# Searching the key lists of all tokens while the queries are made, with 96 instead of 100 first products ahead of the gates

## The chip, the cores and the metric

The kernel runs on one core of a Trainium2 chip, in one launch. The metric is the device time of one execution in microseconds, and the number that counts is the median of several runs. The core has five engines: TensorE (PE in the profile, its weight loads PEld), VectorE (DVE), ScalarE (ACT), GpSimd (POOL) and SyncE (SP), and 16 DMA engines that move data between DRAM and the core's own memory.

## The reference

The function is two transformer blocks on 512 tokens of width 1024, in float32. The first block (attention in a window and a convolution, then a gated feed-forward layer) and the first half of the second (a sparse attention and a spatial gate) are not touched by the change. What matters is the last layer, `peer`, a mixture of 16384 tiny experts:

```
q    = (xn @ wq).reshape(bsz, s, 8, 2, 128)
sub  = einsum('bshpd,hpnd->bshpn', q, subkeys)       # 16 lists of 128 key scores per token
s_top, i_top = top_k(sub, 16)                         # the best 16 of each list
cand = s_top[..., 0, :, None] + s_top[..., 1, None, :]
best, pos = top_k(cand, 16)                           # the best 16 of 256 sums per head
expert = i_top of half 0 * 128 + i_top of half 1, at pos
gate = softmax(best)
a = gelu(x . u_tab[expert]);   y = sum(gate * a * v_tab[expert])
```

Each token thus has 8 heads x 16 = 128 experts out of 16384, and each expert is one row of `u_tab` and one row of `v_tab`, 1024 numbers each.

## The kernel before

Matrix products run in three passes: each operand is split into a rounded part (`whi`, a cast on ScalarE, L138) and the rest (`wlo`, a subtraction on VectorE, L140), and `mm3` (L155 to L158) multiplies high by high, low by high and high by low. `unit` (L132) loads one 128x1024 block of weights on SyncE's queue into `raw` and makes the two parts; all three tiles come from rings of four buffers.

The `peer` layer treats the tokens in two ways. Tokens 0 to 319 (`N_U` = 320) are computed densely: for each of the 128 blocks of 128 experts, `u_block` (L939) forms the first product of all 320 tokens with the block's rows of the first table (8 x 3 matmuls of 320 columns) and applies gelu. The gates for all experts, mostly zero, are built as a dense matrix by `build` (L1091), in 16 steps per 128 tokens: one-hot tiles made by VectorE, multiplied on TensorE (L1117). Later the gated activations of a block meet the block's rows of the second table in `v_block` (L1243), 18 matmuls of 512 columns, the second product. Tokens 320 to 511 are computed sparsely: `gathered` (L954) fetches one row per token and expert by an indirect DMA on GpSimd's queue, and VectorE multiplies and sums it; 64 gathers serve tokens 320 to 383, whose gates are then folded into the dense matrix, and 128 gathers of each table serve tokens 384 to 511.

The layer runs in three stages.

The query stage (L1179 to L1193) is a loop over four rounds (`c4`) of four chunks (`j`). Each chunk is one 128-wide piece of the queries for all 512 tokens (24 matmuls) and its scores against the keys (`skT`). At the end of a round the scores of four lists for each of the four groups of 128 tokens (`tb` 0 to 3) are copied out of the banks to `sub`. `top_keys` (L976) searches one list of one token group: five VectorE instructions over 128x128 scores.

The second stage is the loop of first products made ahead of the gates (L1196 to L1204): `NSPILL` = 100 blocks, chosen by `SPAIR` as pairs spread over the 64 pairs, with the first three pairs left out. Every four results go to DRAM (`a_dram`) and are read back later. Beside them the routing work is issued.

The third stage makes the second products, pair by pair. For a pair in `SPAIR` the first products are read back; for another they are made there and then. The first second product needs the finished gates; the first products of the two opening pairs need none and can run before.

The order of the work is set by generators. `routed` (L1156) yields, after each small piece of routing work, a charge in microseconds; `advance` (L245) draws pieces until a given amount is spent, and stops early at a charge of zero. In the query stage each chunk of rounds 1 to 3 draws `TOP_US`; beside each first product `R_US` is drawn, of which, once the expert numbers of tokens 256 to 383 are known (`ready`), `GATHER` x 2 goes to gathers, and `GATHER` x 1 after the first 64 gathers are issued (`made2`). A search is charged 1.6, `keys` of a group 21.2 (18.7 for the last tokens), a build step 2.7 or 3.4, a gather 1.3. `keys` (L988) selects the best 16 sums of a head and finds the expert numbers; it needs all 16 lists of its group. `routed` takes the lists of `tb` 2 and 3 from `todo` as they come, then runs `keys` of 2 and 3, then searches the 32 lists of `tb` 0 and 1, then `keys` and `build` of 0 and 1, then `build` of 2. What of it is left after the loop is issued behind it (L1205). In the third stage each second product draws `G_US` of gathers, and half as much again where the pair makes its first products there.

The compiler that places the instructions keeps each engine's stream in the order of issue where it can, and lets a later instruction go first where its inputs are ready sooner; searches and the sums over gathered rows are tied behind the last `wlo` issued before them (`pace`).

Of the kernel before, what the change touches and what calls it, by code (L numbers as in the profile page):

```python
# [21 lines left out]
NEG = -1.0e30  # L22
GBUFS = 7

TOP_US = 5.0

R_US = 3.6
GATHER = 0.5
G_US = 2.3
NSPILL = 100  # L30
N_PE_TAPS = (0, 0, 8, 8)
N_GATE = 5
SA_BUFS = 7
# [10 lines left out]

SPAIR = [N_HEAD + i for i in range(64 - N_HEAD) if i * NSPILL // 2 // (64 - N_HEAD) != (i + 1) * NSPILL // 2 // (64 - N_HEAD)]
MAGIC = 1.5 * 2.0 ** 23
# [14 lines left out]
def tile_layers(ctx: ExitStack, tc: tile.TileContext, A: dict, out: bass.AP):  # L61
# [3 lines left out]
    def pool(name, bufs=1, stack=ctx, **kw):  # L65
        return stack.enter_context(tc.tile_pool(name=name, bufs=bufs, **kw))
# [8 lines left out]
    def bank(tag):  # L75
        return ps.tile([128, 512], F32, tag=tag, name="bank_" + tag)
# [51 lines left out]
    def order(ins):  # L128

        return tc.issue_after(ins) if ins is not None else ExitStack()  # L130
# [15 lines left out]
    def next_unit(n=1024, after=(None, None)):  # L146
        u = unit(wt[wpos[0]], n, after)
        wpos[0] += 1
        return u
# [46 lines left out]
    def proj_T(u, xhi, xlo, nk=8, c0=0, o=None):  # L196

        o = bank("a") if o is None else o
        for k in range(nk):
            mm3(o, u[0][:, c0 + k * 128:c0 + (k + 1) * 128], u[1][:, c0 + k * 128:c0 + (k + 1) * 128],  # L200
                xhi[:, :, k, :], xlo[:, :, k, :], k == 0, k == nk - 1)
        return o
# [28 lines left out]
    def chain(*gs):  # L231
        for g_ in gs:
            yield from g_
# [11 lines left out]
    def advance(gen, us):  # L245
        while us > 0:
            c = next(gen, None)
            if c is None:
                return 0.0
            if c == 0.0:  # L250
                return 0.0
            us -= c
        return us
# [685 lines left out]
    def u_block(i1, ap, tag):  # L939

        u = unit(A["ut"][i1])
        o = bank(tag)[:, :N_U]
        for k in range(8):
            mm3(o, u[0][:, k * 128:(k + 1) * 128], u[1][:, k * 128:(k + 1) * 128],
                xhi8[:, k, 0:N_U], xlo8[:, k, 0:N_U], k == 0, k == 7)
        S.activation(ap, o, AF.Gelu_apprx_tanh)
# [29 lines left out]
    def top_keys(sub, tb, hps):  # L976
        sv, si = tops[tb]
        for hp in hps:
            x = sub[:, hp, :]
            with order(pace[0]):  # L980
                V.max(out=sv[:, hp, 0:8], in_=x)
                V.max_index(out=si[:, hp, 0:8], in_max=sv[:, hp, 0:8], in_values=x)
                V.match_replace(out=x, in_to_replace=sv[:, hp, 0:8], in_values=x, imm_value=-3.0e38)
                V.max(out=sv[:, hp, 8:16], in_=x)
                V.max_index(out=si[:, hp, 8:16], in_max=sv[:, hp, 8:16], in_values=x)
            yield 1.6
# [92 lines left out]
    def weights2():  # L1079

        S.activation(zg[64:128, 0:64], ga2[64:128], AF.Gelu_apprx_tanh)
        S.activation(zg[0:64, 64:128], ga2[0:64], AF.Gelu_apprx_tanh)
        zp = bank("b")[:, 0:64]
        T.matmul(zp, zg, fold, start=True, stop=True)
        V.tensor_tensor(gT2, zp, gT2, op=OP.mult)
        for j in range(3):
            V.tensor_copy(w2s[:, j], gT2)
            if j < 2:
                V.tensor_tensor(gT2, gT2, w2s[:, j], op=OP.subtract)
# [38 lines left out]
    with ExitStack() as st:  # L1128
        ptop = pool("ptop", stack=st)
        sTs = {tb: ptop.tile([128, 4, 128], F16, name=f"sT{tb}") for tb in (0, 2)}  # L1130
        sTs[1] = sTs[0]
        gT2 = ptop.tile([128, 64], F32, name="gT2")
        w2s = ptop.tile([128, 3, 64], BF16, name="w2s")
        zg = ptop.tile([128, 128], F32, name="zg")
        G.memset(zg, 0.0)
        fold = ptop.tile([128, 64], F32, name="fold")
        V.tensor_tensor(fold, ident[:, 0:64], ident[:, 64:128], op=OP.add)
        turn16 = ptop.tile([128, 128], F16, name="turn16")
        V.tensor_copy(turn16.rearrange("p (a t) -> p a t", a=2), ident[:, None, 64:128].to_broadcast([128, 2, 64]))
        tops = [(ptop.tile([128, 16, 16], F32, name=f"sv{tb}"), ptop.tile([128, 16, 16], U32, name=f"si{tb}")) for tb in range(4)]  # L1140
        iota16 = ptop.tile([128, 128, 2], F16, name="iota16")
        V.tensor_copy(iota16, cst[:, C_IOTA:C_IOTA + 128][:, :, None].to_broadcast([128, 128, 2]))
        iotab = ptop.tile([128, 16, 128], F16, name="iotab")
        V.tensor_copy(iotab, cst[:, C_IOTA:C_IOTA + 16][:, :, None].to_broadcast([128, 16, 128]))
        ident16 = ptop.tile([128, 128], F16, name="ident16")
        V.tensor_copy(ident16, ident)
        st2 = ExitStack()
        pk = pool("pk", stack=st2)

        sub = [gres[tb].rearrange("p s i t -> p (s i t)")[:, 0:2048].rearrange("p (a n) -> p a n", a=16) if tb < 2 else  # L1150
               pk.tile([128, 16, 128], F32, name=f"sub{tb}") for tb in range(4)]
        skT = pk.tile([128, 16, 128], F32, name="skT")
        nc.scalar.dma_start(skT, A["skT"])
        todo = []

        def routed():  # L1156
            while todo or not keyed:
                if todo:
                    yield from todo.pop(0)
                else:  # L1160
                    yield 0.0
            st2.close()
            pr = pool("pr", stack=st)
            yield from keys(pr, 2)
            yield from keys(pr, 3)
            for tb in (0, 1):
                yield from top_keys(sub[tb], tb, range(16))
            for tb in (0, 1):
                yield from keys(pr, tb)
                yield from build(pr, tb)  # L1170
            while not made2:
                next(gat)
            weights2()
            yield 0.5
            yield from build(pr, 2)

        keyed = []
        route = routed()
        d1 = d2 = 0.0  # L1179
        for c4 in range(4):  # L1180
            sb_ = [bank("b") for _ in range(4)]
            for j in range(4):
                hp = c4 * 4 + j
                qc = pk.tile([128, 512], F32, name="qc", bufs=2)
                S.copy(qc, pr4[j] if c4 == 0 else proj_T(next_unit(), xhi, xlo))
                for tb in range(4):
                    T.matmul(sb_[tb][:, j * 128:(j + 1) * 128], qc[:, tb * 128:(tb + 1) * 128], skT[:, hp, :],
                             start=True, stop=True)
                if c4:
                    d1 = advance(route, d1 + TOP_US)  # L1190
            for tb in range(4):
                S.copy(sub[tb][:, c4 * 4:c4 * 4 + 4, :], sb_[tb].rearrange("p (a n) -> p a n", a=4))
            todo += [top_keys(sub[tb], tb, range(c4 * 4, c4 * 4 + 4)) for tb in (2, 3)]  # L1193
        keyed.append(True)
        for n4 in range(0, 2 * len(SPAIR), 4):
            ab = ptop.tile([128, 4, N_U], F32, name="ab", bufs=2)  # L1196
            for j in range(4):
                u_block(2 * SPAIR[(n4 + j) // 2] + j % 2, ab[:, j, :], "a")

                if ready:  # L1200
                    g1 = GATHER * (2 - len(made2))
                    d2 = advance(gat, d2 + g1)
                d1 = advance(route, d1 + R_US - (g1 if ready else 0.0))
            nc.scalar.dma_start(a_dram[n4 // 4], ab)  # L1204
        for _ in route:  # L1205
            pass
# [196 lines left out]
```

## Time and profile before

| | |
|---|---|
| median of the runs shown | 2115.23 us |
| runs | 2115.23, 3382.32, 2110.91 us |
| profiled execution | 2110.76 us |
| its span, first to last instruction | 2109.0 us |
| mean granted clock of TensorE | 0.989 of full speed |
| busy: TensorE, weight loads, VectorE | 2049.5, 1745.1, 1571.4 us |
| busy: ScalarE, GpSimd | 824.6, 517.9 us |
| DMA | 476.66 MB, mean 226 GB/s |

The profile is one execution; all its times are microseconds from its first instruction. The query stage runs from about 930 to 1025, the second stage from there to about 1465, the third to 2105. A matmul counts as busy until its modelled end, and the next one starts before that, so the distance between starts is the better measure of TensorE's pace. One run of the three, 3382.32 us, is far from the other two.

### The profile page before, as it was taken

What the parts mean: (1) busy time and instruction counts of PE and PEld (TensorE: products, weight loads), DVE (VectorE), ACT (ScalarE), POOL (GpSimd) and SP (SyncE); (2) the same over time, 40 slices, a digit from 0 to 9 for tenths busy, and PEclk for the clock granted to TensorE, in tenths of its full rate; (3) what the DMA queues carried; (4) which work ended last, traced back from release to release, by engine and by line L of the source; (5) the groups of instructions that cost most, each with busy time, mean ns of one, the idle gap of its engine ahead of it and who ended that gap; (6) DMA issues with size and microseconds to landing.
All of it is one profiled execution on the core that took longest, in us unless ns stands there. A gap on an engine that the chain in (4) does not pass through costs nothing.

```text
span 2109.0 us, 29481 instructions
## 1 busy us (share of the span) xinstructions
PE 2049.5 (97%) x11112; PEld 1745.1 (83%) x11112; DVE 1571.4 (75%) x2881; ACT 824.6 (39%) x1339; POOL 517.9 (25%) x383
## 2 busy tenths in 40 slices
PE   7999999999999999999999999999999999999999
PEld 6747888888887777898889899999888878788887
DVE  7974633332279854455789999998899888899997
ACT  5454433222254342333443455555333333233332
POOL 1000000000011000000032212121566666576663
PEclk9999999999999999999999999999999999999999
DMA  5302323333232212342378899999999999999996
GB/s 183 101 21 80 100 93 98 100 112 98 71 104 87 80 59 87 104 145 80 110 282 276 288 326 331 311 359 300 394 399 410 388 400 395 410 395 410 411 404 237
DMA packets 163377, 476.66 MB, mean 226 GB/s; under 512 B 13934, under 2 KB 57326, under 8 KB 161314
## 3 DMA queue, kind: packets, MB, share of 16 engines
q1 hardware_dynamic: 67104, 259.70, 34.5%
q0 software_dynamic: 46752, 169.36, 21.2%
q10 hardware_dynamic: 49378, 45.71, 6.4%
q8 instruction: 87, 1.43, 0.3%
q14 instruction: 56, 0.46, 0.1%
HBM read 431.99 MB, written 42.47 MB: 225 GB/s over the span
## 4 chain that ended last, share of the span: by engine, by line
PE 58%; DVE 26%; issue 6%; DMA 4%; POOL 2%; ACT 2%; DVEq 0%; POOLq 0%; ACTq 0%; SPq 0%
PE bank_a L158 13%; PE bank_a L157 13%; PE bank_a L156 13%; DVE wlo L140 6%; PE bank_b L156 4%; PE bank_b L157 4%; PE bank_b L158 4%; DVE rows L966 2%; DVE rows L958 2%; DMA rows<-in_peer_u_dram,gidx 2%; POOL rows L950 2%; DMA al<-a_dram 1%; DVE mask L708 1%; DVE ohh L1110 1%; DVE oh L1104 1%
## 5 line engine op out<-in xcount | busy, mean ns | idle before, releaser
L138 ACT CAST whi<-raw 128x1024 fp32r<-128x1024 f32 (+1 forms) x413 | 431.9, 1047 | 885.0 <-PE bank_a L157 325.9
L140 DVE TENSOR_TENSOR wlo<-raw,whi 128x1024 fp32r<-128x1024 f32 (+1 forms) x413 | 500.4, 1214 | 268.0 <-ACT whi L138 263.5
L158 PE MATMUL bank_a<-xhi,wlo 128*128 128x320 f32 (+2 forms) x1600 | 545.6, 341 | 5.7 <-DVE wlo L140 3.6
L156 PE MATMUL bank_a<-xhi,whi 128*128 128x320 f32 (+2 forms) x1600 | 549.6, 344 | 1.4 <-issue 1.0
L157 PE MATMUL bank_a<-xlo,whi 128*128 128x320 f32 (+2 forms) x1600 | 546.7, 342 | 2.5 <-DVE xlo L153 2.2
L950 POOL DMA_INDIRECT rows<-in_peer_u_dram,gidx x192 | 277.3, 1444 | 560.4 <-DVE gidx L1051 145.2
L158 PEld LDWEIGHTS bank_a<-xhi,wlo 128*128 128x128 f32 x1600 | 302.3, 189 | 34.7 <-DVE wlo L140 6.3
L157 PEld LDWEIGHTS bank_a<-xlo,whi 128*128 128x128 f32 x1600 | 302.9, 189 | 29.5 <-DVE xlo L153 3.3
L156 PEld LDWEIGHTS bank_a<-xhi,whi 128*128 128x128 f32 x1600 | 302.2, 189 | 28.9 <-issue 2.3
L950 POOL DMA_INDIRECT rows<-in_peer_v_dram,gidx x128 | 205.5, 1606 | 116.4 <-DVE h L973 92.5
L156 PE MATMUL bank_a<-whi,wvhi 128*128 128x512 f32 x512 | 202.0, 394 | 6.3 <-ACT wvhi L152 6.2
L158 PE MATMUL bank_a<-whi,wvlo 128*128 128x512 f32 x512 | 201.6, 394 | 2.4 <-DVE wvlo L153 2.3
L157 PE MATMUL bank_a<-wlo,wvhi 128*128 128x512 f32 x512 | 201.6, 394 | 1.7 <-DVE wlo L140 1.7
L973 DVE SCALAR_TENSOR_TENSOR h<-rows,ga,h 128x1024 f32<-128x1024 f32 x128 | 164.4, 1284 | 5.1 <-DMA rows<-in_peer_v_dram,gidx 3.5
L173 POOL TENSOR_TENSOR rstd<-rstd,neghalf 128x1 f32<-128x1 f32 x20 | 12.2, 612 | 614.1 <-DVE rstd L172 614.1
L966 DVE SCALAR_TENSOR_TENSOR rows<-rows,h 128x1024 f32<-128x1024 f32 x128 | 152.8, 1220 | 8.7 <-DMA rows<-in_peer_u_dram,gidx 8.6
L156 PEld LDWEIGHTS bank_a<-whi,wvhi 128*128 128x128 f32 x512 | 97.0, 189 | 27.6 <-ACT wvhi L152 8.3
L158 PEld LDWEIGHTS bank_a<-whi,wvlo 128*128 128x128 f32 x512 | 97.1, 190 | 26.7 <-DVE wvlo L153 6.1
L157 PEld LDWEIGHTS bank_a<-wlo,wvhi 128*128 128x128 f32 x512 | 97.0, 189 | 21.6 <-DVE wlo L140 2.4
L156 PE MATMUL bank_b<-whi,wvhi 128*128 128x512 f32 x256 | 99.6, 389 | 0.0
L158 PE MATMUL bank_b<-whi,wvlo 128*128 128x512 f32 x256 | 99.6, 389 | 0.0
L157 PE MATMUL bank_b<-wlo,wvhi 128*128 128x512 f32 x256 | 99.6, 389 | 0.0
(402 smaller groups left out, 3269.0 us busy)
## 6 DMA issues: line engine op xcount, KB each, us to landing
raw<-in_wt_dram SPq DMA_DIRECT2D x150, 512.0 KB
raw<-in_ut_dram SPq DMA_DIRECT2D x128, 512.0 KB
raw<-in_peer_v_dram SPq DMA_DIRECT2D x128, 512.0 KB
g_dram<-gt ACTq DMA_DIRECT2D x24, 896.0 KB
gl<-g_dram SPq DMA_DIRECT2D x14, 1536.0 KB
a_dram<-ab ACTq DMA_DIRECT2D x25, 640.0 KB
al<-a_dram SPq DMA_DIRECT2D x25, 640.0 KB
rows<-in_peer_u_dram,gidx POOLq DMA_INDIRECT x192
```

Of the source, the lines that this page charges most:

```text
L138: lead[0] = S.copy(hi[:, :n], raw[:, :n]).ins
L140: pace[0] = V.tensor_tensor(lo[:, :n], raw[:, :n], hi[:, :n].bitcast(F32), op=OP.subtract).ins
L156: T.matmul(o, lh, rh, start=start, stop=False)
L157: T.matmul(o, lh, rl, start=False, stop=False)
L158: T.matmul(o, ll, rh, start=False, stop=stop)
L708: V.match_replace(out=sc, in_to_replace=m8, in_values=sc, imm_value=-3.3e38)
L950: G.indirect_dma_start(out=r, out_offset=None, in_=table, in_offset=bass.IndirectOffsetOnAxis(ap=idx[:, k:k + 1], axis=0))
L958: V.scalar_tensor_tensor(r, r, 1.0, hn2, op0=OP.mult, op1=OP.mult, accum_out=ga2[:, k:k + 1])
L966: V.scalar_tensor_tensor(r, r, 1.0, hn3, op0=OP.mult, op1=OP.mult, accum_out=ga[:, k:k + 1])
L973: V.scalar_tensor_tensor(h[3], r, ga[:, k:k + 1], h[3], op0=OP.mult, op1=OP.add)
L1104: V.tensor_tensor(oh2, io, part(sT[:, 1], t0), op=OP.is_equal)
L1110: V.tensor_tensor(o_, oh2, x_, op=OP.mult)
```

## The change

Four constants change, and the list of waiting searches becomes two lists. After each round the searches of `tb` 2 and 3 go to `todo[0]` and those of `tb` 0 and 1 to `todo[1]`, in pieces of two lists. `routed` draws from the first and, where that is empty, from the second, until the queries are made and the first list is empty; what is then left of the second runs where all 32 searches of `tb` 0 and 1 ran, behind `keys` of 2 and 3. Two pairs leave `SPAIR`, so four first products are made in the third stage.

```diff
-TOP_US = 5.0
-
-R_US = 3.6
-GATHER = 0.5
+TOP_US = 8.0
+
+R_US = 3.3
+GATHER = 0.6
 G_US = 2.3
-NSPILL = 100
+NSPILL = 96
...
-        todo = []
+
+        todo = [[], []]
 
         def routed():
-            while todo or not keyed:
-                if todo:
-                    yield from todo.pop(0)
+            while todo[0] or not keyed:
+                if todo[0] or todo[1]:
+                    yield from (todo[0] or todo[1]).pop(0)
                 else:
                     yield 0.0
             st2.close()
             pr = pool("pr", stack=st)
             yield from keys(pr, 2)
             yield from keys(pr, 3)
-            for tb in (0, 1):
-                yield from top_keys(sub[tb], tb, range(16))
+            yield from chain(*todo[1])
             for tb in (0, 1):
                 yield from keys(pr, tb)
                 yield from build(pr, tb)
...
-            todo += [top_keys(sub[tb], tb, range(c4 * 4, c4 * 4 + 4)) for tb in (2, 3)]
+            for tb in (2, 3, 0, 1):
+                todo[tb < 2] += [top_keys(sub[tb], tb, range(c4 * 4 + j, c4 * 4 + j + 2)) for j in (0, 2)]
```

`chain` runs generators one after the other.

## Rows read from the trace of the kernel before

**Rows 1.** The page's first part: busy us, share of the span, instructions.

```profile
PE 2049.5 (97%) x11112; PEld 1745.1 (83%) x11112; DVE 1571.4 (75%) x2881; ACT 824.6 (39%) x1339; POOL 517.9 (25%) x383
```

**Rows 2.** Table by stretches: length, busy us (instructions), granted clock, DMA share, GB/s.

```profile
core 0: us, PE busy (x) PEld busy (x) DVE busy (x) ACT busy (x) POOL busy (x), PEclk, DMA share, GB/s
945.00:971.00 26.00, 26.00 (x125) 21.18 (x124) 13.32 (x68) 7.09 (x11) 0.00 (x0) 1.00 0.23 77
1045.00:1085.00 40.00, 33.73 (x231) 31.63 (x231) 35.05 (x133) 17.17 (x24) 13.05 (x12) 0.87 0.74 264
1125.00:1225.00 100.00, 94.10 (x674) 90.33 (x673) 99.37 (x337) 44.06 (x65) 22.57 (x20) 1.00 0.83 281
1225.00:1465.00 240.00, 236.13 (x2070) 230.63 (x2068) 234.76 (x414) 136.96 (x250) 49.66 (x39) 0.99 0.97 332
1478.00:2105.00 627.00, 616.60 (x2884) 518.77 (x2883) 570.20 (x648) 211.78 (x238) 384.52 (x240) 0.99 0.98 389
```

**Rows 3.** Timeline of TensorE: start, duration, operation; first and last of even sequences.

```profile
1431.06 0.23 PE L1117 MATMUL bank_b<-oh,ohh 128*128 128x128 f16 x1
...
1432.40 0.22 PE L1117 MATMUL bank_b<-oh,ohm 128*128 128x128 f16 x1
...
1466.10 0.31 PE L156 MATMUL bank_b<-xhi,whi 128*128 128x320 f32 x1
...
1466.98 0.31 PE L156 MATMUL bank_b<-xhi,whi 128*128 128x320 f32 x1
...
1478.42 0.40 PE L156 MATMUL bank_a<-whi,wvhi 128*128 128x512 f32 x1
...
2077.77 0.39 PE L156 MATMUL bank_a<-whi,wvhi 128*128 128x512 f32 x1
...
2079.13 0.39 PE L156 MATMUL bank_b<-whi,wvhi 128*128 128x512 f32 x1
```

**Rows 4.** Timeline of VectorE: two bursts of searches, the first one's end, build operations.

```profile
973.33 0.49 DVE L981 MAX8 sv<-sub 128x8 f32<-128x128 f32 x2 [1.40 <-ACT sub L1192]
...
982.70 2.34 DVE L140 TENSOR_TENSOR wlo<-raw,whi 128x1024 fp32r<-128x1024 f32 x2
...
1025.41 0.49 DVE L981 MAX8 sv<-sub 128x8 f32<-128x128 f32 x2 [1.40 <-ACT sub L1192]
...
1215.70 0.69 DVE L1103 TENSOR_TENSOR oh<-iota,sT 128x1024 f16<-128x1024 f16 x1
...
1216.91 0.69 DVE L1110 TENSOR_TENSOR ohl<-oh,sT 128x1024 f16<-128x1024 f16 x1
```

**Rows 5.** Groups of VectorE instructions, 1025 to 1465: busy us, mean ns, idle before.

```profile
L140 DVE TENSOR_TENSOR wlo<-raw,whi 128x1024 fp32r<-128x1024 f32 x100 | 121.2, 1213 | 4.8 <-ACT whi L138 2.4 <-issue 2.3
L958 DVE SCALAR_TENSOR_TENSOR rows<-rows,h 128x1024 f32<-128x1024 f32 x64 | 77.5, 1214 | 2.0 <-DMA rows<-in_peer_u_dram,gidx 1.9
...
L966 DVE SCALAR_TENSOR_TENSOR rows<-rows,h 128x1024 f32<-128x1024 f32 x6 | 7.3, 1219 | 0.0
```

**Rows 6.** Waits from 930 to 1025: us in total, times, longest.

```profile
DVE wlo L140 <- ACT whi L138: 42.8, 11, 5.3
```

**Rows 7.** Waits from 1025 to 1478.

```profile
ACT whi L138 <- DMA raw<-in_ut_dram: 25.3, 11, 4.1
...
PE bank_b L1043 <- DVE ohl L1040: 7.5, 5, 2.5
```

**Rows 8.** Table by stretches again, three short ones with full DMA engines.

```profile
1250.00:1300.00 50.00, 50.00 (x407) 49.28 (x406) 50.00 (x127) 28.68 (x49) 12.96 (x10) 1.00 1.02 364
1075.00:1085.00 10.00, 6.96 (x24) 5.94 (x25) 7.74 (x24) 2.77 (x4) 5.32 (x5) 0.67 1.03 413
...
1835.00:1850.00 15.00, 10.75 (x35) 7.62 (x34) 14.91 (x14) 5.58 (x7) 9.59 (x6) 0.77 1.03 399
```

**Rows 9.** Waits from 1478 to 2105.

```profile
ACT whi L138 <- DMA raw<-in_peer_v_dram: 104.8, 36, 7.2
...
DVE gl L1237 <- DMA al<-a_dram: 20.3, 5, 4.9
```

## The prediction

> **What bounds the kernel now.** I read the page first: TensorE counts as busy for 97% of the span, VectorE for 75% [rows 1], so only time in which TensorE waits can be won. The table by stage then says where VectorE presses on it [rows 2]. While the queries are made (945 to 1025) TensorE is busy without a gap and VectorE about half the time: 13.32 of 26 us. From 1025 to 1465, the stage of the first products made ahead, VectorE is busy 99.37 of 100 us in the middle and 234.76 of the 240 behind it, and TensorE's gaps lie there. From 1478 on TensorE is at 616.60 of 627 and the DMA engines at 0.98.
>
> A busy share hides spacing, so I priced TensorE by the distance of starts [rows 3]. 320-column products start 0.88 us apart over six, 0.147 each; 512-column ones 1.36 over six, 0.227; the 128-column f16 ones of the gate building 1.34 over 23, 0.058. One first product (24 matmuls) is then 3.52 us. From 1025.4, just behind the last query round, to the first second product at 1478.42 lie 104 of them (100 ahead and four of the two opening pairs), 832 gate matmuls and some 160 of `keys`: 366.1 + 48.3 + 9.3 = 423.7 of 453.0 us. TensorE loses 29 us there. From 1478.4 to 2105 it needs 128 x 18 x 0.227 + 24 x 3.52 = 607 of 627, a loss of 20.
>
> **The change, part by part.**
>
> *Lists moved into the query stage.* A round of four query chunks lasts 26.04 us: the burst of list searches that starts at 973.33 has its like two rounds on, at 1025.41 [rows 4]. Eight searches take 973.33 to 982.70, 9.37 us, 1.17 each. Before, rounds 1 to 3 take 8 each, the lists of tokens 256 to 511. With `TOP_US` 8.0 and 1.6 charged a search, five or six are let out per chunk, so the 16 of a round are out by its third chunk. Then 48 of the 64 searches lie in the query stage instead of 24, and 24 x 1.17 = 28.1 us of VectorE leave the next stage. In a round VectorE gets 16 x 1.17 + 4 x 1.21 (`wlo` subtractions, [rows 5]) = 23.6 us of 26.0: it fits. What is queued behind the burst is the `wlo` of coming chunks, for which TensorE waits. A burst from 973.33 now ends about 992.1; the `wlo` behind it is ready by 993.3, and its chunk starts about 997. The cover is four ring buffers, and 4 us of it are left. I put the cost at 0; if the margin is gone it is about 5 us a round, 10 in all.
>
> The order of what waits for VectorE in that stage speaks for room: in it VectorE stood idle 42.8 us for casts [rows 6].
>
> *Four first products moved behind the gates.* TensorE has 4 x 3.52 = 14.1 us less to do before the first second product and 14.1 more after. VectorE and ScalarE have four splits less ahead, 4.9 us on VectorE. Their four 512 KB loads on SyncE's queue move along, into the stage where ScalarE's casts already waited 104.8 us for table loads [rows 9]; one store of four products on ScalarE's queue and its reload on SyncE's fall away, 640 KB each way.
>
> *The paces.* `R_US` 3.6 to 3.3 and `GATHER` 0.5 to 0.6 only set what is issued beside each first product. In charged units the routing work left after the queries was 12.8 + 21.2 + 18.7 + 51.2 + 128.8 + 49.3 = 282.0; the fourth term drops to 12.8, so 243.6. Before, 100 products paid 9 x 3.6 + 77 x 2.6 + 14 x 3.1 = 276, and one build step came after the loop. After, 96 pay 10 x 3.3 + 69 x 2.1 + 17 x 2.7 = 223.8, and six build steps come behind the loop, about 18 us on VectorE (five operations each, which start 0.605 us apart, [rows 4]). I cost that tail at little: four products of the opening pairs need no gates (14.1 us), and the six steps bring 6 x 24 x 0.058 = 8.4 us of TensorE's own. Gathered rows consumed before the loop ends: 69 x 1.2 / 1.3 + 17 x 0.6 / 1.3, about 72, against 64 + 6 in the trace [rows 5]; two more, 2.4 us, and two gathers fewer on GpSimd's queue behind the gates.
>
> *Sum on VectorE ahead of the second products:* -28.1 - 4.9 + 2.4 = -30.6 us.
>
> *Sum on TensorE.* All its work stays; the gain is only the part of the 29 us of loss that goes. From 1045 to 1085 it is busy 33.73 of 40 at a granted clock of 0.87 [rows 2], about 11 us lost to `keys` of the last tokens and the first gathers. Both stay as they are. The waits of `keys`' matmuls for one-hot tiles, 7.5 us in all [rows 7], stay too. The rest is VectorE being late. Per first product in the gate-building stretches VectorE now has about 2.1/2.7 of a build step of 4 x 0.605, 0.92 gathered rows of 1.21 and a `wlo` of 1.21, together 4.2 us, TensorE 3.52 + 0.7 = 4.2; the two stand level, so a little loss stays. I take 16 us of loss left of 29, a gain of 13.4; ends 0 (VectorE was not the reason) and 22 (all but the `keys` stretch). The first second product then starts 14.1 + 13.4 = 27.5 us sooner, near 1451; VectorE's sum allows 30.6.
>
> *Behind the gates:* +14.1 us for four products, the loss of 20 unchanged. Ends: 0, if they fill gaps, and 24, if two more stalls of the kind at 1835 to 1850 (10.75 of 15 us busy at a granted clock of 0.77, about 5 us, [rows 8]) come with them. I take 14.1, as TensorE's starts there are as close as anywhere.
>
> One rule stands against that value. The Trainium skill's page "Perfetto Trace Analysis", section "Identifying the Most-Contended Engine", holds matmul busy share for a poor measure of TensorE's room and asks for the share of weight loads instead. That share is 518.77 of 627, 83%, in the stretch, which would leave room for the four products. Against it stand the starts of [rows 3], 0.227 apart with nothing between.
>
> Net: -27.5 + 14.1 = -13.4 us. The profiled execution took 2110.76 us, within 0.2 of the lowest run and 4.5 below the median of the runs shown. 2110.76 - 13.4 = 2097; I say 2098.
>
> **Rivals.**
>
> *No gain: transfers, not VectorE, hold the stage.* ScalarE's casts waited 25.3 us for `in_ut` loads [rows 7]. Then the loss of 29 stays, four products change sides, 2111 (2106 to 2116). Against it: VectorE at 99.37 of 100 from 1125 to 1225, with TensorE at 94.10.
>
> *Slower: gathers and loads collide.* The stage runs the same bytes in less time, and gathers go from 0.77 to 0.92 a product. At 1075 to 1085 the first gathers drove the DMA engines to 413 GB/s and share 1.03, and TensorE was busy 6.96 of 10 us at a granted clock of 0.67: about 5 us lost. From 1250 to 1300 the share is already 1.02 at 364 GB/s, with TensorE unharmed [rows 8]. It decides once demand between 1200 and the gates' end passes about 400 GB/s; four such stalls are 20 us, net +7, 2118 (2113 to 2130). The Trainium skill's "DMA: Bandwidth & Descriptors", section "Issuing engines are not separate DMA queues", says that transfers started by SyncE, ScalarE and GpSimd all interleave on the same 16 engines; by it, a gather moved forward is paid by the loads beside it, and the trace at 1075 agrees.
>
> *The four products cost nothing behind the gates.* They sit among 20 us of loss, and waits for reloaded products (20.3 us, [rows 9]) become fewer. Then -27.5 stands, 2083 (2076 to 2090).
>
> *The change does not do what it says:* VectorE's order leaves the moved searches behind the last query chunk. Then only -4.9 + 2.4 ahead and +14.1 behind, 2122.
>
> **How the numbers follow.** Forecast 0.5 (2090 to 2105), no gain 0.2, collision 0.12, free products 0.1, not moved 0.08. The range 2083 to 2117 takes in the first two whole and half of the free products, and leaves out most of the collision and the last: just under 2 in 10. Two per cent, about what a measurement of this kernel can tell from no change, is 42 us. All of TensorE's loss from 1025 on is some 50, so faster by that has 0.03; slower by that would need eight stalls of 5 us, 0.02; within, 0.95.
>
> **What would show it.** In the profile after: 16 searches in one run in each of three query rounds, and TensorE still without a gap there; 16 searches behind 1025; the first second product near 1451; 96 first products ahead and 32 behind; from it to the last matmul about 641 us. It is wrong if TensorE waits for `wlo` before 1025 (margin gone), if the first second product comes later than 1464 (no loss removed), or if the second stage does not grow.

## The result and the profile after

The changed kernel takes 2100.04 us (median of 5 runs, 2098.42 to 2101.43), against 2115.23 us before; the ratio to before, which leaves out the run of 3382.32 us, is 0.9941, with a 95% interval of 0.9929 to 0.9953. The gain is small, 0.6%, but the slowest run of the changed kernel is 8 us below the fastest of before (2109.58). The forecast was 2098 us. The profiled execution has a span of 2098.0 us, 11 less than before.

The table of stretches of the changed kernel, with the columns of [rows 2] (length, busy us of each engine, granted clock, DMA share, GB/s):

```profile
945.00:971.00 26.00, 26.00 (x147) 22.05 (x146) 23.03 (x133) 8.85 (x13) 0.00 (x0) 1.00 0.19 57
...
1045.00:1085.00 40.00, 35.96 (x264) 34.77 (x263) 36.01 (x154) 18.90 (x26) 9.09 (x8) 0.91 0.67 225
1125.00:1225.00 100.00, 96.81 (x752) 95.05 (x751) 99.54 (x241) 51.51 (x82) 27.95 (x23) 0.98 0.92 314
1225.00:1437.00 212.00, 211.44 (x1800) 207.57 (x1799) 198.41 (x332) 120.38 (x212) 44.29 (x36) 1.00 0.97 337
...
1437.00:1465.00 28.00, 22.36 (x207) 20.35 (x205) 22.04 (x32) 12.52 (x24) 4.03 (x3) 1.00 0.73 244
1465.00:2094.00 629.00, 624.82 (x2977) 530.34 (x2975) 570.69 (x647) 217.01 (x246) 383.51 (x238) 1.00 0.98 387
```

While the queries are made VectorE is now busy 23.03 of 26 us instead of 13.32, and TensorE still without a gap. From 1225 TensorE is at 211.44 of 212 and VectorE has room. What is new is the hole from 1437 to 1465. The third stage has the same 0.98 of the DMA engines and hardly a gap of TensorE left, 4 us instead of 10.

One burst of searches on VectorE and the `wlo` behind it, as in [rows 4], and the first matmul of the chunk that needs this `wlo`:

```profile
977.57 0.49 DVE L981 MAX8 sv<-gres 128x8 f32<-128x128 f32 x2 [0.42 <-ACT gres L1192]
...
996.02 1.22 DVE L140 TENSOR_TENSOR wlo<-raw,whi 128x1024 fp32r<-128x1024 f32 x1
...
1000.93 0.40 PE L156 MATMUL bank_a<-xhi,whi 128*128 128x512 f32 x1
```

From the burst's start to the `wlo` are 18.45 us (16 x 1.17 was reckoned), and VectorE's idle time for casts from 930 to 1030 is 18.1 us where [rows 6] has 42.8. Behind 1025 VectorE has 16 searches left instead of 40.

The time of TensorE is compared below by stage, in us. "Ahead" is the number of first products made ahead of the gates. "Second" runs from the start of the last group of score matmuls of the queries to the first second product, "third" from there to the last matmul. "Lost" is the length less the matmuls times the distances of [rows 3], reckoned over the whole timeline; it starts 2 us sooner than the prediction's 29, and so has 32 for the same trace. The first two kernels were traced twice; rows without a median were run once, for the trace. Ratios are to runs of before on the same chip, whose medians were 2111 to 2115 us.

```
kernel                         ahead  second (lost)  third (lost)   median  ratio to before
before                          100   455.1 (32)     626.3 (20)    2115.2
before, second trace            100   452.1 (30)     625.9 (19)
after                            96   436.3 (28)     628.7 (8)     2100.0  0.9941
after, second trace              96   436.6 (28)     632.1 (11)    2099.6  0.9934
lists alone                     100   464.6 (42)     632.2 (25)    2128.8  1.0079
paces and 96 alone               96   466.2 (57)     630.9 (10)    2129.2  1.0091
after, 100 ahead                100   444.9 (23)     630.5 (24)    2107.7  0.9980
after, R_US 3.4                  96   433.9 (25)     631.9 (11)    2098.4  0.9932
after, R_US 3.5                  96   433.6 (25)     634.7 (14)    2096.9  0.9934
after, longer searches           96   439.2 (30)     631.4 (11)    2116.6  1.0017
after, 92 ahead, R_US 3.7        92   416.2 (22)     643.3 (8)     2091.9  0.9900
after, 88 ahead, R_US 3.85       88   412.8 (32)     655.0 (6)     2100.4  0.9945
before, half the gathers        100   454.7 (32)     608.1 (1)
after, half the gathers          96   436.2 (27)     622.4 (2)
```

From before to after the second stage shrinks by 15 to 19 us, the third grows by 2 to 6. The second stage began at 1023.3 and 1028.7 in the two traces of before, at 1028.5 and 1023.8 in those of after: 5 us of chance from the code ahead of it, of which a single pair of spans must be cleared.

### The profile page after: what moved, and what is told of

Its sections match the earlier page's. It is cut to its first block, busy times and chain, and to the rows that moved or that the text cites. A ratio compares the mean times of both kernels' runs of the same rounds, so it can differ in the third digit from the quotient of the medians.

```text
span 2098.0 us, 29475 instructions
## 1 busy us (share of the span) xinstructions
PE 2047.6 (98%) x11112; PEld 1746.2 (83%) x11112; DVE 1574.2 (75%) x2881; ACT 826.4 (39%) x1339; POOL 521.4 (25%) x383
## 5 line engine op out<-in xcount | busy, mean ns | idle before, releaser
L156 PE MATMUL bank_a<-xhi,whi 128*128 128x320 f32 (+2 forms) x1568 | 540.8, 345 | 0.3 <-ACT xhi L152 0.3
L157 PE MATMUL bank_a<-xlo,whi 128*128 128x320 f32 (+2 forms) x1568 | 537.4, 343 | 1.2 <-DVE xlo L153 1.1
L158 PE MATMUL bank_a<-xhi,wlo 128*128 128x320 f32 (+2 forms) x1568 | 534.6, 341 | 0.0
L950 POOL DMA_INDIRECT rows<-in_peer_u_dram,gidx x192 | 283.6, 1477 | 529.6 <-DVE rows L966 161.9
L157 PEld LDWEIGHTS bank_a<-xlo,whi 128*128 128x128 f32 x1568 | 297.6, 190 | 27.5 <-DVE xlo L153 2.3
L156 PEld LDWEIGHTS bank_a<-xhi,whi 128*128 128x128 f32 x1568 | 297.0, 190 | 27.8 <-issue 1.3
L158 PEld LDWEIGHTS bank_a<-xhi,wlo 128*128 128x128 f32 x1568 | 297.3, 190 | 26.2 <-DVE wlo L140 0.4
L156 PE MATMUL bank_b<-xhi,whi 128*128 128x320 f32 (+1 forms) x304 | 99.2, 328 | 2.4 <-ACT xhi L152 2.4
L158 PE MATMUL bank_b<-xhi,wlo 128*128 128x320 f32 (+1 forms) x304 | 98.5, 325 | 1.8 <-DVE wlo L140 1.8
```

What stands on the lines that cost most here:

```text
L156: T.matmul(o, lh, rh, start=start, stop=False)
L157: T.matmul(o, lh, rl, start=False, stop=False)
L158: T.matmul(o, ll, rh, start=False, stop=stop)
L950: G.indirect_dma_start(out=r, out_offset=None, in_=table, in_offset=bass.IndirectOffsetOnAxis(ap=idx[:, k:k + 1], axis=0))
```

## The experiments

The questions were: do the lists or the paces bring the gain; what is lost behind the loop; and why did the third stage not grow by the 14 us of four products?

**Lists alone.** The edit is against the changed kernel:

```diff
 TOP_US = 8.0
-R_US = 3.3
-GATHER = 0.6
+R_US = 3.6
+GATHER = 0.5
-NSPILL = 96
+NSPILL = 100
```

> The moved list searches alone: TOP_US 8.0 and the two lists, with the paces of before (R_US 3.6, GATHER 0.5) and 100 first products ahead. Theory A (VectorE's lateness was the idle time of TensorE in the second stage, and it goes with the 28 us of searches): the stretch from the last query score to the first second product falls from 455 to 440-446 us, no loss at its end (no build step is left behind the loop), and the whole is 2099 to 2107 us. Theory B (the new paces and the 96 products bring the gain, the lists are only moved about): the stretch stays at 450 or more and the time within 4 us of before.

2128.77 us, ratio 1.0079 (1.0064 to 1.0093): 0.8% slower, which neither theory held. The waits from 1325 to 1365 of this kernel (who waited for whom: us, times, longest):

```profile
PE bank_b L1084 <- issue: 13.5, 1, 13.5
ACT zg L1081 <- DVE rows L958: 13.5, 1, 13.5
```

and two stretches of it:

```profile
1325.00:1345.00 20.00, 18.30 (x151) 17.47 (x149) 17.31 (x29) 11.02 (x20) 11.03 (x9) 1.00 1.02 339
1345.00:1365.00 20.00, 6.11 (x38) 5.70 (x39) 17.20 (x33) 1.71 (x4) 12.32 (x10) 0.57 1.03 414
```

The matmul of L1084 folds the gates of tokens 320 to 383 and needs the first 64 gathers. With 24 searches fewer in its way, and drawn at 3.6, routing comes to that point at product 71 by the charges, with 15 of the 64 gathers not yet issued; `routed` then issues them at once. (By the same charges before comes there at product 86 with 4 missing, the changed kernel at 85 with none.) TensorE's stream stood behind the fold for 13.5 us, with the DMA engines full at 414 GB/s. Of the 42 us lost in the second stage 15.6 lie in these two stretches (40 less 24.41 busy); the rest, some 26, is less than the 32 of before. What the lists took away came back at the fold, and the third stage is 6 us longer too, with waits of 3.0 and 1.8 us at pairs 3 and 8 beside those of before. So the pace of the gathers, of which the prediction said that it only sets what is issued beside each product, is a part of the gain.

**Paces and 96 products alone.** The kernel before with `R_US` 3.3, `GATHER` 0.6, `NSPILL` 96.

> The paces and the 96 first products alone (R_US 3.3, GATHER 0.6, NSPILL 96), the searches of tokens 0 to 255 left where they were. By the charges 57 us of routing are then left behind the loop instead of 20. Theory A (VectorE's relief pays for the faster pace): TensorE stands idle behind the loop for some 57 x 0.9 - 14 (products that need no gates) - 12 (its own build matmuls) = 25 us, and the kernel is slower than before, 2118 to 2135 us. Theory B (the gain is in the paces and the products moved): 2097 to 2105 us.

2129.22 us, 1.0091 (1.0076 to 1.0106), as theory A has it. By the distances 32 us are lost between 1424 and 1484 behind the loop, where 25 were reckoned:

```profile
1420.00:1490.00 70.00, 50.43 (x477) 42.53 (x474) 60.05 (x98) 33.35 (x69) 4.03 (x3) 0.80 0.63 202
```

Each half alone makes the kernel slower. With the searches left in place the new paces leave 19 build steps behind the loop by the charges, with them moved six.

**The loss behind the loop: `R_US` 3.5 and 3.4.** The only line changed:

```diff
-R_US = 3.3
+R_US = 3.5
```

> The changed kernel with R_US 3.5 instead of 3.3: by the charges no build step is left behind the loop of first products, where the changed kernel leaves six. Theory A (the 8 us that TensorE loses between 1428 and 1465 in the changed kernel are those six steps, run on VectorE with too little beside them): that loss falls to 2 us or less, the stretch to the first second product from 436 to 429-432, the whole 2092 to 2097 us. Theory B (the loss is the wait for the gates as such, or comes back as VectorE being late in the build stretches): 436 +- 2 and 2098 to 2102 us.

> The changed kernel with R_US 3.4: three build steps are left behind the loop instead of six. Theory A (the loss behind the loop goes with the steps left there): that loss falls from 8 to about 4 us; what VectorE then owes earlier (a faster draw of routing beside each product) costs 0 to 3 us in the build stretches; the whole 2094 to 2100 us. Theory B: no change, within 1 us of the changed kernel, as between R_US 3.3 and 3.5.

TensorE's timeline of the changed kernel behind the loop (start, duration, idle before and what ended it):

```profile
1439.38 0.29 PE L1117 MATMUL bank_b<-oh,ohh 128*128 128x128 f16 x2 [1.62 <-DVE ohh L1110]
1439.98 0.29 PE L1117 MATMUL bank_b<-oh,ohl 128*128 128x128 f16 x2 [0.31 <-DVE ohl L1110]
1440.58 0.23 PE L1117 MATMUL bank_b<-oh,ohm 128*128 128x128 f16 x1 [0.31 <-DVE ohm L1110]
1442.51 0.29 PE L1117 MATMUL bank_b<-oh,ohh 128*128 128x128 f16 x2 [0.61 <-DVE ohh L1110]
...
1449.48 0.39 PE L156 MATMUL bank_b<-xhi,whi 128*128 128x320 f32 x1
```

Build step follows build step every 3.1 us, each waiting for its one-hot tiles, and the first of the four opening products starts at 1449.48, behind the last of them. With 3.5 nothing is left there and TensorE is busy without a gap (the same kernel with 3.5, the 20 us ahead of its first second product):

```profile
1437.00:1457.00 20.00, 20.00 (x165) 19.90 (x163) 10.35 (x14) 10.01 (x17) 2.88 (x3) 1.00 0.86 272
```

The loss behind the loop is 8.5 us at 3.3, 5.0 at 3.4, 0.3 at 3.5: it goes with the steps left there, as theory A has it. The second stage gains only 2 to 3 us of it, as theory B has it in part; with 3.5 more is lost at its start (13 us between 1043 and 1123 instead of 10 to 11) and at the `keys` behind it (about 6 us between 1143 and 1183 instead of 5, and 1.6 near 1270). Its length of 433.6 lies between the ranges of the two theories. On the whole nothing is gained: 0.9934 (0.9919 to 0.9949) with 3.5 and 0.9932 (0.9915 to 0.9949) with 3.4 are not apart from the 0.9934 of the changed kernel's second timing.

**The stalls of the third stage: before again, after again, 100 ahead.**

> The kernel before once more, for a second trace. Theory A (the two stalls of TensorE in the third stage, 13 of its 19.5 us of loss, belong to the order of transfers of this kernel): the loss from the first second product to the last is 15 to 24 us again, with stalls at the same two pairs. Theory B (they are chance of one execution): the loss is under 12 us or the stalls lie elsewhere. The 5.2 us by which the unchanged stretch before the queries was shorter than in the trace of the changed kernel should not repeat exactly: 1018 to 1030 for the last query score.

> The changed kernel once more, for a second trace and times on one chip with the next kernels. Theory A (where its losses lie is settled by its order of work): the second stage is 434 to 439 us with some 8 us lost behind the loop, the third 627 to 631 us without a stall at pairs 25 and 36, the whole 2096 to 2104 us. Theory B (chance of one execution): stages off by more than 5 us, or the loss behind the loop under 4 us.

> The changed kernel with 100 first products ahead again (NSPILL 100), lists and paces as changed. Theory A (the third stage grew by 2.4 us instead of 14.1 because with 96 products the two stalls at pairs 25 and 36 are gone, while the products themselves cost their full 14): the third stage is 624 to 629 us with the stalls back at pairs 25 and 36; the second is 436 + 14 less some 4 (three build steps behind the loop instead of six), 443 to 450; the whole 2101 to 2108 us. Theory B (the products fill gaps behind the gates, the stalls had another cause): the third stage is 612 to 618 us and the whole 2092 to 2098.

The stalls repeat. In the trace of before, VectorE waits 4.03 us for a reload of first products (`al`), and TensorE then waits at the start of pair 36:

```profile
1833.48 0.82 DVE L1237 TENSOR_TENSOR gl<-al,gl 128x640 f32<-128x640 f32 x1 [4.03 <-DMA al<-a_dram]
...
1840.46 0.39 PE L158 MATMUL bank_b<-whi,wvlo 128*128 128x512 f32 x1
1844.50 0.80 PE L156 MATMUL bank_a<-whi,wvhi 128*128 128x512 f32 x1 [3.65 <-ACT wvhi L152]
```

and in its second trace:

```profile
1847.28 0.50 PE L156 MATMUL bank_a<-whi,wvhi 128*128 128x512 f32 x1 [3.66 <-ACT wvhi L152]
```

The kernel with the lists alone, also with 100 ahead, stalls at pair 36 as well (3.6 us of wait) and at pair 25 (2.5 in all three). The kernels with 96 ahead (both traces of after, the paces alone, `R_US` 3.4 and 3.5) wait at neither; the longest wait that they share is 1.4 to 3.0 us at pair 40. With 100 ahead again the third stage is 630.5 us long, 1.5 above theory A's range and 12 above B's, with 24 us lost: waits of 2.5 and 1.7 us at 25 and 36, and of 3.3 and 1.1 at 8 and 52 too. The pairs are no accident: in every kernel of the table the waits of over 1 us for `wvhi` fall on pairs that `SPAIR` leaves out at that number, 8, 25, 36 and 52 with 100 ahead, 7, 12 and 40 with 96, and 3 with any, so on pairs whose first products are made in the third stage. With 96 the waits went to other such pairs and are shorter: 2.4 and 3.0 us in the two traces of after, 6.2 in both of before. The second stage is 444.9, as forecast. The whole is 2107.70 us, 0.9980 (0.9970 to 0.9991): four products on the other side of the gates take back most of the gain. The second trace of after agrees with theory A, its third stage 1 us above the range.

**Half the gathers left out.** In both kernels the fetches of odd `k` for tokens 384 to 511 are left out, in both tables; VectorE takes the row fetched before once more, so the results of those tokens lack half their rows:

```diff
-            r = gather(A["peer_u"], gidx, k)
+            r = gather(A["peer_u"], gidx, k) if k % 2 == 0 else r
...
-            r = gather(A["peer_v"], gidx, k)
+            r = gather(A["peer_v"], gidx, k) if k % 2 == 0 else r
```

> The kernel before with every second gather of tokens 384 to 511 left out (both tables; VectorE uses the row fetched before it again). About 125 of 250 transfers of 512 KB leave the third stage, VectorE's work stays. Theory A (full DMA engines delay the reloaded products, and that is the two stalls): the loss of TensorE from the first second product to the last falls from 19 to 3 us or less, the stage from 626 to 607-611 us. Theory B (the stalls come from the order of VectorE's or ScalarE's work): the stalls at pairs 25 and 36 stay, 620 us or more.

> The changed kernel with the same gathers left out. Theory A (with the DMA engines relieved TensorE sets the third stage in both, so the four products show their price there): 621 to 625 us, 13 to 15 more than the kernel before with the same gathers left out. Theory B (the products are free, they fill waiting time): within 4 us of it.

The third stage of before with half the gathers:

```profile
1481.00:2089.00 608.00, 608.00 (x2880) 516.72 (x2878) 568.21 (x648) 211.97 (x238) 187.16 (x117) 1.00 0.82 292
```

and of after:

```profile
1462.00:2085.00 623.00, 623.00 (x2981) 531.63 (x2979) 571.09 (x648) 217.64 (x246) 183.63 (x116) 1.00 0.80 286
```

VectorE and ScalarE do the same work as with all gathers ([rows 2] and the table above); GpSimd issues half as many, and the DMA engines went from 0.98 to 0.82 and 0.80. TensorE loses 1 to 2 us. So the stalls hang on transfers that came late; whether these were the loads, the reloads or the gathered rows themselves is left open. The four products cost 622.4 - 608.1 = 14.3 us, the 14.1 of the prediction. (One run each, of 2094.82 and 2091.10 us.)

**Longer searches.** Four more `FIND_INDEX8` in each search of tokens 0 to 255, with the same result:

```diff
                 V.max_index(out=si[:, hp, 8:16], in_max=sv[:, hp, 8:16], in_values=x)
+                for _ in range(4 if tb < 2 else 0):
+                    V.max_index(out=si[:, hp, 8:16], in_max=sv[:, hp, 8:16], in_values=x)
```

> The changed kernel with four more FIND_INDEX8 in each search of tokens 0 to 255 (the same result written again), about 1.04 us a search; the charges stay. It takes the margin in the query stage away: a round then asks VectorE for 16 x 1.17 + 8 x 1.04 + 4 x 1.21 = 31.9 us of 26.0. Theory A (the cover of four ring buffers, 4 us, is what made the moved lists free): TensorE waits for wlo in rounds 2 and 3, the stretch to the last query score grows by 4 to 12 us, the second stage by 3 to 8, the whole is 2106 to 2122 us. Theory B (the searches would slip behind the queries and leave TensorE alone): no gap before the last query score, and 28 us more of VectorE in the second stage, the whole 2112 to 2130 us.

2116.64 us, 1.0017 (1.0006 to 1.0027), as theory A has it. The rounds of this kernel:

```profile
945.00:971.00 26.00, 26.00 (x136) 21.61 (x136) 24.58 (x167) 7.80 (x12) 0.00 (x0) 1.00 0.11 39
971.00:997.00 26.00, 23.55 (x108) 19.00 (x107) 26.00 (x157) 7.42 (x11) 0.00 (x0) 0.93 0.24 82
997.00:1025.00 28.00, 24.04 (x109) 19.52 (x108) 27.05 (x164) 7.41 (x12) 0.00 (x0) 0.88 0.22 76
```

and its waits from 930 to 1041:

```profile
PE bank_a L158 <- DVE wlo L140: 10.1, 3, 4.0
```

From the first score matmul to the last the query stage takes 98.4 us here and 83.3 in both before and after: 15 more, above the 4 to 12 forecast. The waits are 10.1 of them, and the granted clock, 0.93 and 0.88, is lower in the rounds with waits. The second stage is only 3 us longer. The searches do not slip back behind the queries; what made them free was the margin. A burst of this kernel overruns both the cover of the ring buffers and a round's room on VectorE (31.9 of 26 us), so the run does not tell which of the two ends first.

**Fewer ahead: 92 and 88.** The edit for 92; with 88 `R_US` is 3.85 and `GATHER` 0.7.

```diff
-R_US = 3.3
-GATHER = 0.6
+R_US = 3.7
+GATHER = 0.65
-NSPILL = 96
+NSPILL = 92
```

> The changed kernel with 92 first products ahead, R_US 3.7 and GATHER 0.65: four more products move behind the gates, no build step is left behind the loop and no gather is forced by the charges. Theory A (all TensorE work is constant, only its idle time counts; behind the gates more products per gathered byte relieve the DMA engines): second stage 436 - 14 - up to 8 = 414 to 422 us, third 628.7 + 14 - 0 to 4 = 638 to 643, the whole 2088 to 2096 us. Theory B (VectorE sets the second stage: it has only four splits less to do, 5 us): second stage 428 us or more, the whole 2100 to 2108.

> The changed kernel with 88 first products ahead, R_US 3.85 and GATHER 0.7 (75 gathered rows ahead by the charges, no step left behind the loop). In the kernel with 92, VectorE is busy 403 of the 416 us of the second stage. Theory A (VectorE is the floor of that stage now): four splits less (5 us) against one to three gathered rows more (1 to 4 us), so 411 to 417 us instead of 402; the third grows by 14 less up to 3, to 654 to 658; the whole 2098 to 2108 us, slower than with 92. Theory B (TensorE's idle time still has room to go): 400 to 406 and 654 to 658, the whole 2088 to 2094.

With 92: 2091.89 us, 0.9900 (0.9883 to 0.9916), the fastest of all. The second stage is 416.2, as theory A said, the third 643.3, at the upper end of its range. VectorE is now close to full in the second stage (stretches of the kernel with 92, then the second stage of the one with 88):

```profile
1026.00:1086.00 60.00, 53.94 (x392) 51.19 (x392) 56.20 (x255) 30.87 (x44) 13.73 (x13) 1.00 0.62 220
1086.00:1206.00 120.00, 118.09 (x922) 113.87 (x921) 120.00 (x300) 65.33 (x103) 33.70 (x28) 1.00 0.92 323
1206.00:1428.00 222.00, 220.28 (x1896) 212.89 (x1895) 216.84 (x389) 123.97 (x224) 49.09 (x41) 1.00 0.99 342
...
1026.00:1437.00 411.00, 396.10 (x3195) 379.34 (x3194) 393.51 (x944) 218.91 (x366) 106.42 (x83) 0.99 0.90 314
```

With 88 theory A's floor shows: 412.8 instead of the 402 that four products less would give, with VectorE busy 393.51 of 411 us and TensorE 396.10; 655.0 behind, 2100.36 us, 0.9945 (0.9932 to 0.9959). Of the numbers tried 92 is the best. That the best lies where TensorE's and VectorE's work ahead of the gates are alike fits this, but the paces were changed along with the numbers and no run separates the two.

## Why the prediction was right, step by step

**What bounds the kernel** was read rightly: TensorE's work is constant, and only its idle time moves. With all gathers in, the kernels of the table differ by the two columns of loss and by chance, and by nothing else of size (before loses 52 us in the two stages, after 36, the kernel with 92 ahead 30), but for the one with longer searches, which loses its time while the queries are made.

**The moved searches are free**, as reckoned: TensorE has no gap ahead of 1025, a burst takes 18.45 us, and the `wlo` behind it is done by 997.24, 3.7 us ahead of the start of its chunk at 1000.93. The cover was put at 4 us, from a chunk that "starts about 997"; in the trace of before that chunk starts at 995.70, so the figure is right in part by luck. The longer searches show that the margin is real and what lies beyond it. Losing it was put at 5 us a round and 10 in all; there the waits are 10.1 us, and 15 with the lower clock.

**The second stage** was to shrink by 27.5 us, 14.1 for the four products and 13.4 of loss, and shrank by 15 to 19: the loss went from 32 and 30 to 28. The step that failed is "I cost that tail at little: four products of the opening pairs need no gates (14.1 us), and the six steps bring 6 x 24 x 0.058 = 8.4 us of TensorE's own". The opening products stand behind the build steps in TensorE's stream, so they cover nothing of VectorE's time there: 8.5 us lost. The rest of the loss, 19 us, is near the 16 that was taken: 10 at the start, as said, and about 5 at the first `keys` behind it. But the tail is not simply to be had back: with `R_US` 3.5 it is gone, and the loss is still 25, since the steps are then drawn sooner and VectorE is late elsewhere.

**The third stage** was to grow by 14.1 us with its loss of 20 unchanged; it grew by 2 to 6, and its loss is 8 to 11. The mis-sized term is "the loss of 20 unchanged". Its two large stalls stand in all three kernels with 100 ahead, at pairs that make their first products there; with 96 other pairs do, and the waits are shorter. All but 1 of the 20 us go when the DMA engines get room. The price of the products was right, 14.3 against 14.1. So the rival of free products has the sum of that stage nearly right by another way: the products are not free, other waits went. The Trainium skill's page "Perfetto Trace Analysis", section "Identifying the Most-Contended Engine", judges TensorE's room by the share of weight loads and, beside it, by the share of peak arithmetic, which was not reckoned here. The trace does not bear out the first of the two: with the gathers halved, weight loads took 85% of the third stage (516.72 of 608 us), and yet each further product cost its full time. The distances of [rows 3] are the better measure here.

**The total** came out within 2 us by luck, since the two misses, 9 to 12 us too hopeful ahead and 8 to 12 too gloomy behind, cancel. The gain of some 13 us is shown; that it would come out of these two terms was not foreseen. Two of the signs say the same: the first second product was to come near 1451, with the prediction wrong beyond 1464, and came at 1464.86 and, in the second trace, at 1460.4 (in the first the stage also began 5 us late by chance); and the third stage, forecast at about 641 us, took 628.7 and 632.1. The range, too, was a little narrower than its own chances: half of the free products, most of the collision and the unmoved lists come to about 0.22, not just under 0.2.

**The rivals.** That nothing is gained is out. The collision of gathers and loads did not come in the changed kernel (0.97 of the DMA engines from 1225 to 1437 and 211.44 of 212 for TensorE), but the lists alone ran into something like it, by another door: gathers issued all at once because routing had run ahead of them. That the change does not do what it says is out: only 16 searches are left behind 1025.

What stays open is why, with 100 ahead, the waits are long at pairs 25 and 36 and not at the other pairs that make their first products there, which transfer is the late one, and why the loss at the start of the second stage is 10 us in one kernel and 13 in another.

## What to carry to other kernels

When one engine's work is constant and full, add up its idle time by stage, and treat each edit as moving idle time, not work: a term that is "unchanged loss" has to be looked at as hard as the term that changes. A cover counts only if it stands ahead of the wait in the covering engine's own stream; free work that is issued later covered nothing here. Pace constants that draw side work belong to the amount of side work: here changing one without the other gave a tail of 32 us or a forced burst of 13.5.

## What the runs showed of the hardware

A wait cost TensorE more than its length. Behind the wait of 3.65 us at pair 36 the granted clock was 0.50, the level of 1.2 GHz, for 5 us:

```profile
1844.50:1849.50 5.00, 5.00 (x11) 3.59 (x12) 5.00 (x6) 3.31 (x4) 2.61 (x2) 0.50 1.00 397
```

The 12 matmuls of 512 columns from 1844.50 on took 5.46 us, start to start, where the distance of [rows 3] gives 12 x 0.227 = 2.72. Over the 20 us of the 13.5 us wait in the kernel with the lists alone the mean granted clock was 0.57.

The DMA engines at a share of 0.98 and 389 GB/s came with a loss of 20 us of 626 on TensorE in before; at 0.82 and 292 GB/s, with half the gathers and the same work on every computing engine but GpSimd, which issues them, the loss was 1 us. In after the share is 0.98 too, at 387 GB/s, and the loss 8 to 11: the mean share does not tell how much is lost.
